# Stacked two-pass scores, masks combined later, a shorter gate series and later attention parts in a one-core hybrid layer

## The chip, the cores and the metric

The kernel runs on one core of one Trainium2 chip. The metric is the device time of one execution in microseconds (us). Before the change it was 987.21, 987.92 and 988.73 us in three runs, with a median of 987.92.

## The reference

One layer serves a prompt of 512 rows and a sample group of 64 rows (576 columns in all) with the same weights, D = 1024:

```python
h = x + concat(gated_delta(n), diff_attention(n)) @ w_out      # n = rmsnorm(x), one projection n @ w_in feeds both
h = h + mem_attention(rmsnorm(h), mem_k, mem_v)                # mem_k, mem_v = rmsnorm(mem) @ w_mem_k, w_mem_v
h = h + square(relu(rmsnorm(h) @ w_ff1)) @ w_ff2
```

Two pieces matter for the change. The gates of the gated-delta part are g = -exp(a_log) * softplus(a + dt_bias) and beta = sigmoid(b). In the differential attention, each of 4 heads has two components c of width 64; a query of component c meets the keys of component c, two softmaxes result, and a = p0 - lam * p1 multiplies the values. Queries come in blocks of 128 and see the keys up to the end of their own chunk of 64. The sample rows see 256 cached keys and their own 64.

## The kernel before

The work is transposed: features lie on the 128 partitions, tokens (576) in the free dimension. `project` (L162 to L165 belong to its weight loading) multiplies 128 columns of weights with all tokens. To keep fp32 accuracy, `split_weights` divides the weights `raw` into a rounded part `wh` (ACT, L161) and a rest `wl` (DVE, L162), both fp32r, and activations are divided likewise; a product is three fp32r matmuls, issued by `mm` (L107) into a PSUM bank `pr`. `tr` (L113) transposes on TensorE. Banks: `pr` has 3, `ba` 2, `g0`, `g1` and `gs` one each, so that a matmul into `g0` waits until all readers of the last content of `g0` are done.

The stages, in time order: norm of x; projection and convolution of 12 blocks of gated-delta inputs (to about 105 us; evacuation in `conv_input`, L322 and L323; Silu at L459 and L460); gates (L507 to L590); the remaining projection `z`, with five chunks of the gated-delta recurrence woven in (to about 250 us; Silu of `z` at L647 and L649); differential attention (to about 355 us); memory K and V, output projection, memory attention, feed-forward (to the end).

The gates: L507 gathers `ab2`, L522 to L526 form t = exp(-|pre|), L527 to L534 a series for log(1 + t), L535 to L538 give `gg`. Triangular matmuls turn `gg` into cumulated sums `Gc`, `kdc` (an exp at L571) and `kdc2` (L590). A DRAM round trip (`gdram` L577, `grow` L582) gives rows of the sums broadcast over the partitions.

`gdn_prep` prepares a chunk: transposes of k into `g0` or `g1`, `kd` from them (DVE, L680), their squares (ACT, L682) and sums (DVE, L683); the same for q (L686, L687), a power on GpSimd (`rpow`, L208), decays `Y` from `grow` or from a matmul (L700, exp at L701), then `At` (L705), `KQ` (L709) and `vb` (L717). It uses `lev`, a matrix of powers of two made from seven masks (L605 to L614; three GpSimd instructions and two DVE instructions for each mask).

`diff_project` projects q, k and v of a head. q goes into `qz`, 128 rows by 2 components, with zeros in the rows of the other component; so a score is one fp32 matmul of `qz` with all 128 rows of k (`kdT`), in `diff_head`, L1019 being the maximum of a row. `finish` norms a head's output into `od`, which is split into `ob` (L201, L202) behind the memory keys.

The order of each engine's instructions is fixed at build time by the framework's scheduler, which takes the code's order as priority and its own estimates of durations; tile buffers, their counts and `issue_after` bound it. Weights come over SP's DMA queue in the order that it was given too. Two of ScalarE's functions, exp and Silu, use different tables; where they alternate, the compiler puts an ACT_TABLE_LOAD between.

Of the kernel before, what the change touches and what calls it, by code (L numbers as in the profile page):

```python
# [15 lines left out]
P = 128  # L16
D = 1024
KT = 8
SEQ = 512
# [18 lines left out]
def hybrid_layer_kernel(  # L38
# [53 lines left out]
    def small(tag, shape, bufs=None, dt=F32):  # L92
        tag = SHARED.get(tag, tag)
        bufs = 1 if tag in ("vn", "on", "S") or tag[:-1] in ("At", "Dt", "Y") else 2
        return sp.tile(shape, dt, tag=tag, name=nm(tag), bufs=bufs)
# [216 lines left out]
    def conv_input(m, tag="cb"):  # L312
# [3 lines left out]
        def evac(b, a0, n, more):  # L316
# [4 lines left out]
            else:  # L321
                A.copy(cb[:, 3 + a0 : 259 + a0], b[:, :256])  # L322
                V.tensor_copy(cb[:, SOFF + 3 : SOFF + 3 + DEC], b[:, 256:])  # L323
# [206 lines left out]
    V.tensor_scalar(t3, t2, 1.0 / 17, 1.0 / 15, ALU.mult, ALU.add)  # L530
    for d in (13, 11, 9, 7, 5, 3, 1):
        V.tensor_tensor(t3, t3, t2, ALU.mult)
        V.tensor_scalar(t3, t3, 1.0 / d, None, ALU.add)
    V.tensor_tensor(t3, t3, t1, ALU.mult)  # L534
# [64 lines left out]
    with tc.issue_after(behind_keys[0]), tc.issue_after(behind_keys[1]):  # L599
        lev = const([P, P], "lev")  # L600
        prev = ident
        for lb in range(7):
            s = 2 << lb
            e = small("X", [P, P])
# [4 lines left out]
            m = small("B0", [P, P])  # L609
            V.tensor_tensor(m, e, prev, ALU.subtract)  # L610
            if lb == 0:
                V.tensor_copy(lev, m)
            else:
                V.scalar_tensor_tensor(lev, m, float(1 << lb), lev, ALU.mult, ALU.add)  # L614
            prev = e
# [323 lines left out]
    qz = [cp.tile([P, 2, T], F32, tag=f"qz{i}", name=f"qz{i}") for i in range(2)]  # L939
    with tc.issue_after(behind_keys[0]), tc.issue_after(behind_keys[1]):  # L940
        for q2 in qz:
            G.memset(q2[64:, 0, :], 0.0)
            G.memset(q2[:64, 1, :], 0.0)
        G.memset(vs[64:], 0.0)

    def diff_project(h):
        hs = slice(h * P, (h + 1) * P)
        for kind, base in (("q", 2056), ("k", 2568), ("v", 3080)):
            def evac(b, a0, n, more):
                ts_ = slice(a0, a0 + n)  # L950
                if kind == "q":
                    for c in range(2):
                        R = slice(64 * c, 64 * c + 64)
                        if more is not None:
                            add_to(qz[h % 2][R, c, ts_], b[R], more[R])
                        else:
                            (A.copy if c else V.tensor_copy)(qz[h % 2][R, c, ts_], b[R])
                    return
# [664 lines left out]
```

## Time and profile before

| | |
|---|---|
| time, three runs | 987.21, 987.92, 988.73 us |
| profiled execution | 987.2 us |
| its span | 985.5 us |
| TensorE busy | 968.5 us (98%) |
| DVE busy | 699.7 us (71%) |
| ACT busy | 530.1 us (54%) |
| granted TensorE clock | 0.997 |

Times in the trace are from the start of the span; about 1.7 us of the execution lie outside it. PE is TensorE, DVE VectorE, ACT ScalarE, POOL GpSimd, SP SyncE. A row of the timeline has its start, its duration, engine, line, operation, out<-in, shape, the number of instructions merged, and in brackets how long the engine had stood idle before it and what it waited for. PE's durations overlap; what counts is the distance of starts.

### The profile page before, as it was taken

To read this page: it belongs to the slowest core of one execution; us is meant where nothing else is said; L and a number is where in the kernel's file an instruction comes from. 1 tells how busy PE (TensorE), PEld (TensorE's weight loads), DVE (VectorE), ACT (ScalarE), POOL (GpSimd) and SP (SyncE) were. 2 spreads that over 40 slices of the span, in tenths; PEclk is the share of its full clock that TensorE was granted. 3 is DMA by queue.
4 is the path that set the end of the run, shared out by engine and by line. 5 is a ranking of instruction groups with operands and counts; after the bars stand their busy time and mean duration, and the time that the engine had idled before them with its cause. 6 is when DMAs were issued, how large, how long until landed. Compare 5 with 4: busy or idle time off the path is not lost.

```text
span 985.5 us, 16923 instructions
## 1 busy us (share of the span) xinstructions
PE 968.5 (98%) x6403; PEld 891.2 (90%) x6403; DVE 699.7 (71%) x1570; ACT 530.1 (54%) x1194; POOL 58.8 (6%) x127
## 2 busy tenths in 40 slices
PE   9999999999999999999999999999999999999996
PEld 7989899898888878999999999999999999999996
DVE  6666787877676676666557977657867779978674
ACT  7545575344656665444445657665544445555444
POOL 3341011101000000000000000000000000000000
PEclk9999999999999999999999999999999999999998
DMA  7432340103222647333111414222222223223202
GB/s 212 129 119 65 90 138 23 43 23 103 81 68 68 203 131 227 95 94 99 44 44 58 127 54 127 86 86 86 86 87 86 86 86 86 86 86 86 65 23 96
DMA packets 121714, 90.75 MB, mean 92 GB/s; under 512 B 5564, under 2 KB 112206, under 8 KB 121122
## 3 DMA queue, kind: packets, MB, share of 16 engines
q1 hardware_dynamic: 121266, 89.03, 30.9%
q8 instruction: 50, 0.82, 0.3%
q10 hardware_dynamic: 368, 0.66, 0.2%
q14 instruction: 30, 0.25, 0.1%
HBM read 79.93 MB, written 9.75 MB: 91 GB/s over the span
## 4 chain that ended last, share of the span: by engine, by line
PE 83%; DVE 4%; issue 3%; POOL 2%; DMA 2%; ACT 2%; POOLq 0%; ACTq 0%; SPq 0%; DVEq 0%
PE pr L107 51%; PE g L107 12%; PE ba L107 10%; PE gs L107 6%; PE ba L113 3%; PE g L113 1%; POOL tg L208 1%; DMA r<-in_w_ff_dram 1%; DVE p L457 1%; DVE wl L162 0%; DMA grow<-gdram 0%; DMA raw<-in_w_ff_dram 0%; POOL X L607 0%; POOL X L608 0%; DVE on L809 0%
## 5 line engine op out<-in xcount | busy, mean ns | idle before, releaser
L107 PE MATMUL pr<-u,wh 128*128 128x320 f32 (+2 forms) x1240 | 328.7, 343 | 1.3 <-DVE p L323 1.2
L107 PEld LDWEIGHTS pr<-u,wh 128*128 128x128 f32 x1240 | 212.3, 188 | 18.0 <-DVE p L323 1.8
L107 PE MATMUL pr<-u,wl 128*128 128x256 f32 (+1 forms) x816 | 226.7, 302 | 0.0
L107 PEld LDWEIGHTS pr<-u,wl 128*128 128x128 f32 x816 | 149.9, 189 | 2.7 <-DVE wl L388 0.2
L162 DVE TENSOR_TENSOR wl<-raw,wh 128x1024 fp32r<-128x1024 f32 x65 | 79.4, 1223 | 41.3 <-ACT wh L161 41.0
L161 ACT CAST wh<-raw 128x1024 fp32r<-128x1024 f32 x65 | 68.1, 1048 | 65.7 <-PE pr L107 50.5
L107 PE MATMUL pr<-u,w2h 128*128 128x320 f32 (+1 forms) x384 | 98.5, 340 | 0.0
L1369 ACT CAST w2h<-r 128x512 fp32r<-128x512 f32 x56 | 34.7, 620 | 87.9 <-PE pr L107 85.3
L107 PE MATMUL pr<-f,w2h 128*128 128x320 f32 (+1 forms) x288 | 74.3, 340 | 0.1
L107 PEld LDWEIGHTS pr<-u,w2h 128*128 128x128 f32 x384 | 65.0, 188 | 4.5 <-ACT u L1452 0.3
L107 PE MATMUL pr<-u,w2l 128*128 128x256 f32 (+1 forms) x256 | 65.1, 295 | 0.0
L1454 DVE TENSOR_TENSOR u<-u,pr 128x256 f32<-128x256 f32 x96 | 42.3, 448 | 16.9 <-PE pr L107 16.2
L107 PE MATMUL ba<-u,wl 128*128 128x288 f32 x360 | 53.0, 296 | 0.4 <-ACT keep L1405 0.4
L107 PEld LDWEIGHTS pr<-f,w2h 128*128 128x128 f32 x288 | 48.7, 188 | 4.0 <-issue 1.1
L107 PEld LDWEIGHTS ba<-u,wl 128*128 128x128 f32 x360 | 49.2, 188 | 1.2 <-ACT keep L1405 1.1
L107 PE MATMUL pr<-f,w2l 128*128 128x256 f32 (+1 forms) x192 | 48.8, 295 | 0.0
L107 PEld LDWEIGHTS pr<-u,w2l 128*128 128x128 f32 x256 | 46.9, 188 | 1.5
L208 POOL TENSOR_TENSOR tiny<-tiny,nhalf 128x1 f32<-128x1 f32 (+4 forms) x10 | 8.7, 870 | 631.6 <-DVE tiny L1522 529.8
L1370 DVE TENSOR_TENSOR w2l<-r,w2h 128x512 fp32r<-128x512 f32 x56 | 38.5, 688 | 10.7 <-ACT w2h L1369 10.4
L107 PE MATMUL pr<-wh,u 128*128 128x512 f32 x128 | 41.4, 401 | 0.0
L1414 ACT ACTIVATE c<-c 128x288 f32<-128x288 f32 x48 | 20.6, 443 | 29.5 <-DVE c L1413 29.5
L107 PEld LDWEIGHTS pr<-f,w2l 128*128 128x128 f32 x192 | 35.2, 188 | 1.2
(514 smaller groups left out, 2025.1 us busy)
## 6 DMA issues: line engine op xcount, KB each, us to landing
raw<-in_w_ff_dram SPq DMA_DIRECT2D x36, 512.0 KB
raw<-in_w_in_dram SPq DMA_DIRECT2D x28, 512.0 KB
r<-in_w_ff_dram SPq DMA_DIRECT2D x56, 256.0 KB
raw<-in_w_mem_k_dram SPq DMA_DIRECT2D x8, 512.0 KB
raw<-in_w_mem_v_dram SPq DMA_DIRECT2D x8, 512.0 KB
raw<-in_w_out_dram SPq DMA_DIRECT2D x8, 512.0 KB
raw<-in_w_mem_q_dram SPq DMA_DIRECT2D x8, 512.0 KB
raw<-in_w_mem_o_dram SPq DMA_DIRECT2D x8, 512.0 KB
```

Of the source, the lines that this page charges most:

```text
L107: i = nc.tensor.matmul(out, lhsT, rhs, start=start, stop=stop, skip_group_check=skip_group_check)
L113: i = nc.tensor.transpose(out, in_, ident[:n, :n])
L161: A.copy(wh, raw)
L162: V.tensor_tensor(wl, raw, wh.bitcast(F32), ALU.subtract)
L208: G.tensor_tensor(out, in_, bc(nhalf[: in_.shape[0], 0:1], list(in_.shape)), ALU.pow)
L457: V.scalar_tensor_tensor(yv[:, :n], cb[:, i : i + n], cwt[:, m, i : i + 1], yv[:, :n], ALU.mult, ALU.add)
L1369: A.copy(wh, src)
L1370: V.tensor_tensor(wl, src, wh.bitcast(F32), ALU.subtract)
L1414: A.activation(c, c, AF.Relu)
L1454: V.tensor_tensor(am, am, b, ALU.add)
```

## The change

Five edits go together. Scores of the prompt are made by two fp32r matmuls: the rounded part and the rest of q stand in the upper and lower 64 rows of `qs`, and one component's k, rounded part and rest, each stand twice, in both halves of the partitions; the stacking is done by DMAs from SBUF to SBUF, and the buffers are taken from tags that are free by then. `qz` holds only the last 128 columns, for the sample rows. The small evacuation at L323 moves to ACT. The gates' series loses seven instructions. The masks of `lev` are made ahead in two `X` tiles, and are combined later, with 7 DVE instructions in place of 14. The split of the attention output into `ob` stands in the code behind the first half of the memory values.

```diff
@@ -91,7 +91,7 @@
 
     def small(tag, shape, bufs=None, dt=F32):
         tag = SHARED.get(tag, tag)
-        bufs = 1 if tag in ("vn", "on", "S") or tag[:-1] in ("At", "Dt", "Y") else 2
+        bufs = 1 if tag in ("vn", "on", "S", "qz") or tag[:-1] in ("At", "Dt", "Y") else 2
         return sp.tile(shape, dt, tag=tag, name=nm(tag), bufs=bufs)
 
     def tiny(shape, tag="tiny", bufs=16):
@@ -320,7 +320,7 @@
                 add_to(cb[:, 3:259], b, more)
             else:
                 A.copy(cb[:, 3 + a0 : 259 + a0], b[:, :256])
-                V.tensor_copy(cb[:, SOFF + 3 : SOFF + 3 + DEC], b[:, 256:])
+                A.copy(cb[:, SOFF + 3 : SOFF + 3 + DEC], b[:, 256:])
 
         return evac
 
@@ -527,11 +527,10 @@
     V.reciprocal(t2, t2)
     V.tensor_tensor(t1, t1, t2, ALU.mult)
     V.tensor_tensor(t2, t1, t1, ALU.mult)
-    V.tensor_scalar(t3, t2, 1.0 / 17, 1.0 / 15, ALU.mult, ALU.add)
-    for d in (13, 11, 9, 7, 5, 3, 1):
-        V.tensor_tensor(t3, t3, t2, ALU.mult)
-        V.tensor_scalar(t3, t3, 1.0 / d, None, ALU.add)
-    V.tensor_tensor(t3, t3, t1, ALU.mult)
+    V.tensor_scalar(t3, t2, 1.0 / 17, None, ALU.mult)
+    for d in (15, 13, 11, 9, 7, 5, 3):
+        V.scalar_tensor_tensor(t3, t3, 1.0 / d, t2, ALU.add, ALU.mult)
+    V.scalar_tensor_tensor(t3, t3, 1.0, t1, ALU.add, ALU.mult)
     V.tensor_scalar(pre, pre, 0.0, None, ALU.max)
     V.scalar_tensor_tensor(t3, t3, 2.0, pre, ALU.mult, ALU.add)
     V.tensor_tensor(t3, t3, ea.unsqueeze(1).to_broadcast([P, 5, 4]), ALU.mult)
@@ -596,23 +595,19 @@
     mn = view(e5, 0, 2, D)
     mhl = pair(4, F32R)
     mh, ml = view(mhl, 0, KT, NMEM), view(mhl, 1, KT, NMEM)
-    with tc.issue_after(behind_keys[0]), tc.issue_after(behind_keys[1]):
-        lev = const([P, P], "lev")
-        prev = ident
-        for lb in range(7):
+    near_ = [t for u in (small("X", [P, 4, P]), small("X", [P, 4, P])) for t in (u[:, 0, :], u[:, 1, :], u[:, 2, :])]
+    with tc.issue_after(behind_keys[1]):
+        for lb, e in enumerate(near_):
             s = 2 << lb
-            e = small("X", [P, P])
             G.memset(e, 1.0)
             ev = e.rearrange("p (n s) -> p n s", s=s)
             G.affine_select(out=ev, in_=ev, pattern=[[-s, P // s], [0, s]], compare_op=ALU.is_ge, fill=0.0, base=0, channel_multiplier=1)
             G.affine_select(out=ev, in_=ev, pattern=[[s, P // s], [0, s]], compare_op=ALU.is_ge, fill=0.0, base=s - 1, channel_multiplier=-1)
-            m = small("B0", [P, P])
-            V.tensor_tensor(m, e, prev, ALU.subtract)
-            if lb == 0:
-                V.tensor_copy(lev, m)
-            else:
-                V.scalar_tensor_tensor(lev, m, float(1 << lb), lev, ALU.mult, ALU.add)
-            prev = e
+    lev = const([P, P], "lev")
+    with tc.issue_after(last_v):
+        V.tensor_scalar(lev, ident, -1.0, 64.0, ALU.mult, ALU.add)
+        for lb, e in enumerate(near_):
+            V.scalar_tensor_tensor(lev, e, -float(1 << lb), lev, ALU.mult, ALU.add)
 
 
 
@@ -936,31 +931,62 @@
     cv2 = view(e3, 1, 4, 4 * P).rearrange("p (i b) n -> p i b n", i=2)
     ckT, cvv = cv2[:, 0].rearrange("p b (c n) -> p (b c) n", n=PAST), cv2[:, 1]
 
-    qz = [cp.tile([P, 2, T], F32, tag=f"qz{i}", name=f"qz{i}") for i in range(2)]
+    qs = [cp.tile([P, 2, T], F32R, tag=f"qz{i}", name=nm("qs")) for i in range(2)]
+    qz = small("qz", [P, 2, P])
     with tc.issue_after(behind_keys[0]), tc.issue_after(behind_keys[1]):
-        for q2 in qz:
-            G.memset(q2[64:, 0, :], 0.0)
-            G.memset(q2[:64, 1, :], 0.0)
+        G.memset(qz[64:, 0, :], 0.0)
+        G.memset(qz[:64, 1, :], 0.0)
         G.memset(vs[64:], 0.0)
+    stacked = {}
 
     def diff_project(h):
         hs = slice(h * P, (h + 1) * P)
+        if h < 2:
+            qn = [od[:, 2 * h + j, :SEQ].bitcast(F32R) for j in range(2)]
+        else:
+            qn = [small(tag, [P, SEQ], dt=F32R) for tag in ("Y0", "Y1")]
+        tags = ("kd", "vb", "X", "KQ") if h % 2 else ("At0", "At1", "Dt0", "Dt1")
+        ks = [small(tag, [P, SEQ], dt=F32R) for tag in tags]
+        stacked[h] = ks[:2], ks[2:]
         for kind, base in (("q", 2056), ("k", 2568), ("v", 3080)):
             def evac(b, a0, n, more):
                 ts_ = slice(a0, a0 + n)
+                t0 = slice(a0, min(a0 + n, SEQ))
+                n0 = t0.stop - a0
+
+                def parts(dst, src):
+                    A.copy(dst[0][:, t0], src[:, :n0])
+                    V.tensor_tensor(dst[1][:, t0], src[:, :n0], dst[0][:, t0].bitcast(F32), ALU.subtract)
+
                 if kind == "q":
-                    for c in range(2):
-                        R = slice(64 * c, 64 * c + 64)
-                        if more is not None:
-                            add_to(qz[h % 2][R, c, ts_], b[R], more[R])
-                        else:
-                            (A.copy if c else V.tensor_copy)(qz[h % 2][R, c, ts_], b[R])
+                    d = b
+                    if more is not None:
+                        d = qn[1][:, ts_].bitcast(F32)
+                        add_to(d, b, more)
+                    parts(qn, d)
+                    if a0:
+                        for c in range(2):
+                            R = slice(64 * c, 64 * c + 64)
+                            A.copy(qz[R, c, :], d[R, n - P :])
+                            for j in range(2):
+                                nc.sync.dma_start(
+                                    qs[h % 2][64 * j : 64 * j + 64, c, :SEQ].bitcast(F32), qn[j][R].bitcast(F32)
+                                )
                     return
                 d = small("zr", [P, 320])[:, :n] if kind == "v" else kdT[:, h, ts_]
                 if more is not None:
                     add_to(d, b, more)
                 else:
                     V.tensor_copy(d, b)
+                if kind == "k":
+                    parts(stacked[h][0], d)
+                    if a0:
+                        first_, second_ = ([x.bitcast(F32) for x in pair_] for pair_ in stacked[h])
+                        for j in range(2):
+                            for R in (slice(0, 64), slice(64, P)):
+                                nc.sync.dma_start(second_[j][R], first_[j][64:])
+                        for j in range(2):
+                            nc.sync.dma_start(first_[j][64:], first_[j][:64])
                 bt = bank()
                 for t in range(2):
                     tr(bt[:, t * P : (t + 1) * P], d[:, t * P : (t + 1) * P])
@@ -1005,22 +1031,22 @@
             q0 = QT[t][0]
             nk = q0 + P if t < 4 else PAST + DEC
             nb = (nk + P - 1) // P
-            pr = []
+            pr = {}
             mx, l = tiny([P, 2], "ta"), tiny([P, 2], "ta")
-            for c in range(2):
+            for c in (1, 0):
                 b = bank(f"g{c}")
-                qq = qz[h % 2][:, c, q0 : q0 + P]
                 if t < 4:
-                    mm(b[:, :nk], qq, kdT[:, h, :nk])
+                    for j in range(2):
+                        mm(b[:, :nk], qs[h % 2][:, c, q0 : q0 + P], stacked[h][c][j][:, :nk], start=j == 0, stop=j == 1)
                     V.memset(b[:64, nk - 64 : nk], -1e30)
                 else:
-                    mm(b[:, :PAST], qq, ckT[:, h, :])
-                    mm(b[:, PAST:nk], qq, kdT[:, h, SEQ:T])
+                    mm(b[:, :PAST], qz[:, c, :], ckT[:, h, :])
+                    mm(b[:, PAST:nk], qz[:, c, :], kdT[:, h, SEQ:T])
                 V.tensor_reduce(mx[:, c : c + 1], b[:, :nk], AX.X, ALU.max)
                 V.tensor_scalar(mx[:, c : c + 1], mx[:, c : c + 1], -0.125, None, ALU.mult)
                 p = small(f"p{c}", [P, 512])
                 A.activation(p[:, :nk], b[:, :nk], AF.Exp, bias=mx[:, c : c + 1], scale=0.125, accum_out=l[:, c : c + 1])
-                pr.append(p)
+                pr[c] = p
             V.reciprocal(l, l)
             V.tensor_tensor(l[:, 1:2], l[:, 1:2], nlam, ALU.mult)
             V.tensor_scalar(pr[1][:, :nk], pr[1][:, :nk], l[:, 1:2], None, ALU.mult)
@@ -1109,7 +1135,7 @@
             nc.sync.dma_start(out[0, 0].rearrange("(b p) h d -> p b (h d)", p=P)[:, :, fs], dst[:, :, fs])
             if out is o_mk and f == 1:
                 finish()
-
+            if out is o_mv and f == 0:
                 ob = pair(5, F32R)
                 for h in range(H):
                     split_to((ob,), od[:, h, :], h, 0)
```

New line numbers in the gates and in `gdn_prep` are 1 lower (L570 for L571, L589 for L590) and 5 lower (L675 for L680, L695 for L700).

The first place is DVE around the gates. In `gg_1158` and the like the last number is a tile's own. Before, from the last step of the series on:

```order
L537 TENSOR_TENSOR t3_1162<-t3_1162,tiny_136_1155 128x20
L538 TENSOR_SCALAR gg_1158<-t3_1162 128x20
L545 COPY gg2_1191<-gg_1158 64x2 x2
L548 MEMSET gg_1158 64x4
L568 COPY Gc_1233<-ba_143_1230 128x20
...
L570 TENSOR_TENSOR kdc_1235<-ba_143_1230,Gc_1233 128x20
...
L680 TENSOR_TENSOR kd_167_1315<-g0_166_1310,kdc_1235 128x512
L680 TENSOR_TENSOR kd_208_1485<-g1_207_1480,kdc_1235 128x512
L162 TENSOR_TENSOR wl_272_1851<-raw_270_1848,wh_271_1850 128x1024
L683 TENSOR_REDUCE tg_165_1309<-B0_168_1317 128x4
L700 SCALAR_TENSOR_TENSOR Y1_213_1503<-grow_146_1246,Gc_1233,most1_1101 128x128 x2
```

After, the same stretch, from the end of `gg` on:

```order
L537 TENSOR_SCALAR gg_1158<-t3_1162 128x20
...
L547 MEMSET gg_1158 64x4
...
L569 TENSOR_TENSOR kdc_1228<-ba_143_1223,Gc_1226 128x20
L162 TENSOR_TENSOR wl_260_1822<-raw_258_1819,wh_259_1821 128x1024
L695 SCALAR_TENSOR_TENSOR Y1_201_1474<-grow_146_1239,Gc_1226,most1_1101 128x128 x2
L675 TENSOR_TENSOR kd_155_1286<-g0_154_1281,kdc_1228 128x512
L675 TENSOR_TENSOR kd_196_1456<-g1_195_1451,kdc_1228 128x512
...
L678 TENSOR_REDUCE tg_153_1280<-B0_156_1288 128x4
L682 TENSOR_REDUCE tg_153_1280<-B0_158_1296 128x4
...
L707 TENSOR_TENSOR tg_167_1333<-tg_153_1280,tg_152_1279 128x4
...
L695 SCALAR_TENSOR_TENSOR Y0_161_1309<-g0_160_1304,Gc_1226,most1_1101 128x128 x4
```

`kd` stood ahead of the decays `Y1` from `grow` and now stands behind the first two of them; the decays `Y0` stand behind L707, which reads GpSimd's power.

The second place is ACT behind the gates. Before:

```order
L549 ACT_TABLE_LOAD
L549 ACTIVATE t1_1160<-ab_1150 128x20
L569 ACTIVATE egl_1234<-ba_143_1230 128x20
L571 ACTIVATE kdc_1235<-kdc_1235 128x20
L590 ACTIVATE kdc2_1194<-kdc2_1194 128x2
L161 CAST wh_271_1850<-raw_270_1848 128x1024
L682 ACTIVATE B0_168_1317<-g0_166_1310 128x512
```

After:

```order
L568 ACTIVATE egl_1227<-ba_143_1223 128x20
L589 ACTIVATE kdc2_1187<-kdc2_1187 128x2
L644 ACT_TABLE_LOAD
L644 ACTIVATE u_2_76<-pr_247_1686 128x64
L161 CAST wh_259_1821<-raw_258_1819 128x1024
L570 ACT_TABLE_LOAD
L570 ACTIVATE kdc_1228<-kdc_1228 128x20
L194 COPY u_2_76<-pr_251_1719 128x256
L642 ACT_TABLE_LOAD
L642 ACTIVATE u_2_76<-pr_252_1739 128x256
L677 ACTIVATE B0_156_1288<-g0_154_1281 128x512
```

The exps of `egl`, `kdc` and `kdc2` stood together behind one table load; now Silu's of `z` stand between them and in front of the squares `B0`, each change with a load. From the gates' first exp (L525) to the end of the first chunk's `At` there are 12 loads, where there were 6.

The third place is SP's DMA queue where head 0 and head 1 of the differential attention meet. `At0`, `At1` hold head 0's k (component 0, rounded part and rest), `Dt0`, `Dt1` component 1; `kd_516`, `vb_517`, `X_518`, `KQ_519` are the same for head 1. Before:

```order
L977 DMA out_2_dram<-p0_455_2694 128x2x128
L980 DMA out_8_dram<-p0_455_2694 64x128
L990 DMA p0_468_2773<-in_cache_diff_k_dram 128x512
L1179 DMA B0_884_4940<-in_cache_mem_v_dram 128x512
L988 DMA u_2_76<-in_cache_diff_v_dram 128x2x512
```

After:

```order
L989 DMA At1_434_2550<-At1_434_2550 64x512
L1014 DMA u_2_76<-in_cache_diff_v_dram 128x2x512
L987 DMA Dt0_435_2551<-At0_433_2549 64x512 x2
L987 DMA X_518_2955<-kd_516_2953 64x512
L1009 DMA out_3_dram<-u_4_78 128x4x128
L1010 DMA out_9_dram<-vs_2542 64x128
L989 DMA At0_433_2549<-At0_433_2549 64x512
L987 DMA X_518_2955<-kd_516_2953 64x512
L987 DMA KQ_519_2956<-vb_517_2954 64x512 x2
L157 DMA raw_684_3762<-in_w_in_dram 128x8x128
```

The copies of k stand between the outputs and the weights; head 0's last copy stands behind the first copy of head 1.

## The prediction

> **What bounds the kernel.** I read the page first: busy shares, then the chain that ended last.
>
> ```profile
> PE 968.5 (98%) x6403; PEld 891.2 (90%) x6403; DVE 699.7 (71%) x1570; ACT 530.1 (54%) x1194; POOL 58.8 (6%) x127
> ...
> PE 83%; DVE 4%; issue 3%; POOL 2%; DMA 2%; ACT 2%; POOLq 0%; ACTq 0%; SPq 0%; DVEq 0%
> ```
>
> TensorE works 98% of 985.5 us and carries 83% of the chain. So two things alone move the time: matmul time, and moments in which TensorE stands still. Next the stages that the change touches (columns: PE, weight load, DVE, ACT, POOL busy), and TensorE's waits there (total, times, longest).
>
> ```profile
> 102.00:118.00 16.00, 15.54 (x103) 13.61 (x103) 12.53 (x44) 9.03 (x15) 0.00 (x0) 1.00 0.42 113
> 117.00:135.00 18.00, 17.36 (x120) 15.76 (x121) 14.60 (x47) 14.19 (x27) 3.32 (x2) 1.00 0.49 156
> 250.00:355.00 105.00, 104.06 (x610) 86.45 (x609) 72.64 (x239) 62.95 (x207) 4.78 (x7) 1.00 0.32 99
> ```
>
> ```profile
> PE pr L107 <- DVE p L323: 1.2, 2, 1.0
> ...
> PE pr L107 <- DVE wl L162: 0.8, 1, 0.8
> ...
> PE g L113 <- DVE KQ L709: 0.5, 1, 0.5
> ...
> PE ba L107 <- DVE gg L548: 0.5, 1, 0.5
> ```
>
> In the differential-attention stage (250 to 355) TensorE idles 0.9 us of 105: matmul time saved there counts in full. In the gate stage (102 to 135) it idles 1.1 us, with DVE at about 80% and ACT at 79% of 117 to 135: there little room is left, and whatever makes their results late stops TensorE.
>
> **Part 1, the scores: -7.1 us.** The score matmuls now run in fp32 and become two fp32r matmuls with stacked halves.
>
> ```profile
> 264.88 0.28 PE L107 MATMUL pr<-u,wl 128*128 128x256 f32 x1
> 265.00 0.40 PE L107 MATMUL pr<-u,wh 128*128 128x512 f32 x1
> 265.24 0.40 PE L107 MATMUL pr<-u,wl 128*128 128x256 f32 x2
> ...
> 265.71 1.04 PE L107 MATMUL g<-u,qz 128*128 128x512 f32 x2
> 266.58 0.38 PE L113 MATMUL ba<-ident,p 128*128 128x128 f32 x2
> ```
>
> ```profile
> L107 PE MATMUL g<-u,qz 128*128 128x512 f32 x16 | 8.4, 609 | 0.0
> L107 PE MATMUL g<-u,qz 128*128 128x384 f32 x16 | 7.0, 519 | 0.0
> ```
>
> One fp32 matmul is two instructions (the form of 512 columns has 16 for 8 matmuls). From start to start the pair takes 0.87 us (265.71 to 266.58), 0.85 ns per column and instruction; an fp32r instruction of 512 columns takes 0.24 us and one of 256 0.12 (265.00 to 265.24, 264.88 to 265.00), 0.46 ns per column. The new form has as many instructions, so it saves 0.39 ns per column: 16 x (512+384+256) columns x 0.39 = 7.1 us. For t=0 (128 columns) I count nothing: bounds 0 and 16 x 128 x 0.39 = 0.8 us. The sample scores (t=4) stay fp32.
>
> The price is paid elsewhere: per head two more casts and two subtractions for q and k each, and two copies into `qz`.
>
> ```profile
> L194 ACT COPY zr<-pr 128x256 f32<-128x256 f32 x12 | 4.5, 374 | 10.1 <-PE pr L107 10.1
> ...
> L195 DVE TENSOR_TENSOR zr<-pr,zr 128x256 f32<-128x256 f32 x12 | 5.1, 422 | 2.5 <-ACT zr L194 2.3
> ```
>
> That is 4 x 0.37 on ACT and 4 x 0.42 on DVE per head, less what the old evacuation took, some 5 us and 3 us in all; against 42 and 32 us free in 250 to 355 it is hidden, and without that cover it would cost these 8 us. New too are 40 copies from SBUF to SBUF on SP's queue. Their landing isn't in this trace; the nearest rows:
>
> ```profile
> 118.45 0.28 SPq L577 DMA_DIRECT2D gdram<-p  x1
> 119.77 0.35 SPq L582 DMA_DIRECT2D grow<-gdram  x1
> ...
> 123.81 0.62 DVE L700 SCALAR_TENSOR_TENSOR Y<-grow,Gc,most 128x128 f32<-128x128 f32 x2 [0.91 <-DMA grow<-gdram]
> ```
>
> 10 KB had landed 1.3 us after issue, 256 KB 4.0 us after. Tightest is head 0: its last k copy stands on SP behind head 1's first (the third pair of order blocks shows it), which waits for head 1's k. From that evacuation 1.3 us, four issues of 0.4 and a landing make 4.2 to 6.9 us; the matmuls that stand before its first score take 7.4. The other copies that it waits for can add a landing. Behind these copies SP still has the next weights to fetch (`raw_684`), which are first split well over 4.0 us later and wait no longer than the scores do. So 0 to 1.6 us, and I take 0.5, nearer the covered end, as the order leaves room.
>
> **Part 2, the conv evacuation: -1.2 us.** The 64-column copy moves from DVE to ACT.
>
> ```profile
> 57.56 1.22 DVE L162 TENSOR_TENSOR wl<-raw,wh 128x1024 fp32r<-128x1024 f32 x1
> ...
> 58.69 0.22 DVE L323 COPY p<-pr 128x64 f32<-128x64 f32 x1
> ...
> 58.97 0.50 PE L107 MATMUL pr<-u,wh 128*128 128x512 f32 x1 [1.04 <-DVE p L323]
> ```
>
> It stood behind a weight split and masks' subtractions; ACT is idle there, so both waits (1.2 in all) go. Masks now need no subtraction and stand later. The lower bound is 0.2, should ACT's own queue be late.
>
> **Part 3, attention parts later: -0.3 us.** The one wait on `wl` in the memory stage:
>
> ```profile
> 361.80 1.42 DVE L202 TENSOR_TENSOR u<-u,u 128x576 fp32r<-128x576 f32 x2
> 363.14 2.35 DVE L162 TENSOR_TENSOR wl<-raw,wh 128x1024 fp32r<-128x1024 f32 x2
> ```
>
> The wait is 0.8 us behind those splits. In the new order three of four splits still stand ahead of a `wl` that TensorE reaches after 6.1 us of matmuls instead of 5.9, so most of it stays: 0 to 0.8, I take 0.3.
>
> **Part 4, the gate stage: +7.8 us.** Here the order changes most. T is the moment at which `gg` is ready.
>
> ```profile
> 106.15 0.24 DVE L507 COPY ab<-ba 128x80 f32<-128x80 f32 x1 [0.30 <-PE ba L113]
> ...
> 111.60 0.18 DVE L532 TENSOR_TENSOR t<-t,t 128x20 f32<-128x20 f32 x1
> 111.81 0.18 DVE L533 TENSOR_SCALAR t<-t 128x20 f32<-128x20 f32 x1
> ...
> 117.04 0.06 DVE L548 MEMSET gg<- 64x4 f32 x1
> ```
>
> ```profile
> 117.16 0.40 PE L107 MATMUL ba<-gg,triu 128*128 128x20 f32 x2 [0.46 <-DVE gg L548]
> ...
> 135.10 0.60 PE L113 MATMUL g<-ident,X 128*128 128x128 f32 x4
> ```
>
> The series loses 7 instructions of 0.21 us (111.60 to 111.81), 1.5 us; `lev` puts 7 of about 0.29 in, three quarters of which fall into gaps in which DVE waited for ACT. `gg` comes 10.1 us after L507 instead of 10.95. But TensorE reaches it 13 matmuls of 320 columns earlier (0.46 ns x 320 = 0.147 each, 1.9 in all): it waits 0.46 + 1.9 - 0.9 = 1.5 us.
>
> Behind T, ACT alternates between exp and Silu, each time with a table load:
>
> ```profile
> 108.44 1.28 ACT L525 ACT_TABLE_LOAD   x1
> 109.73 0.22 ACT L525 ACTIVATE t<-t 128x20 f32<-128x20 f32 x1
> ...
> 118.75 0.22 ACT L571 ACTIVATE kdc<-kdc 128x20 f32<-128x20 f32 x1 [0.53 <-DVE kdc L570]
> 119.89 0.20 ACT L590 ACTIVATE kdc<-kdc 128x2 f32<-128x2 f32 x1 [0.93 <-DVE kdc L589]
> 120.00 1.04 ACT L161 CAST wh<-raw 128x1024 fp32r<-128x1024 f32 x1
> ```
>
> Before, `kdc` was there at T+1.9 (118.97). Now it follows `kdc2` (T+2.8), a load (1.28), a Silu (0.2), a cast (1.04), a load and its exp: T+6.8. On DVE its user, `kd`, stands moreover behind `Y1`, which waits for `grow` at T+6.7 (123.81 less 117.10) and takes 0.6: both `kd` end at T+8.6 instead of T+4.0. On ACT a copy, a third load and a Silu put the k squares at T+9.4. TensorE needs that bank at T+7.0 (matmuls between by the pitches above): **2.4 us**. A fourth load puts the q squares at T+12.2, sums and POOL's power at T+14.9:
>
> ```profile
> 125.20 0.17 DVE L688 TENSOR_SCALAR tg<-tg 128x8 f32<-128x8 f32 x1
> ...
> 127.14 0.16 DVE L712 TENSOR_TENSOR tg<-tg,tg 128x4 f32<-128x4 f32 x1 [0.42 <-POOL tg L208]
> ```
>
> (1.94 us between the two). `Y0`'s four decays, now behind that step, end at T+16.2, wanted at T+14.9: **1.3**. The scaled memory rows (L233), behind the second pair of sums and POOL, end at T+19.8, wanted at T+17.7: **2.1**. `At0`'s last part stands behind a `wl` (1.2): T+22.2 against T+20.8: **1.4**. `KQ` at T+24.7 against T+23.0: **1.7**. Together 8.9, with `gg` 10.4, less the 0.9 that stood here before: 9.5. Adding starts instead: TensorE is at `gg` at 116.7 - 1.2 - 1.9 = 113.6, waits 1.5, and 26.2 us behind T reaches the transposes of `X` that stood at 135.10. There it has ten matmuls of `pr_261` (five of 512 columns, five of 256) and two of 320 more still to do, 2.05 us, but eight transposes (0.9) less: 113.6 + 1.5 + 26.2 + 1.15 - 135.1 = 7.3, or 8.5 without part 2's 1.2. In such hand sums some waits cover one another, so I take 7.8; bounds 3.5 (`kd` and the squares alone, 2.4, with `gg`'s rise of 1.1) and 10.
>
> [...]
>
> **Sum.** -7.1 + 0.5 - 1.2 - 0.3 + 7.8 = -0.3. The profiled execution took 987.2 us (span 985.5 and 1.7 around it): 986.9. The median of the runs, 987.92, is 0.7 above it: 987.6. The bounds of the terms give -7.1 -0.8 -1.2 -0.8 +3.5 = -6.4 (981.5) and -7.1 +1.6 -0.2 +10 = +4.3 (992.2).
>
> **Rivals.**
> - *The gate waits cover one another* (faster). If TensorE's first stop lets DVE and ACT catch up, only the lower bound, 3.5, is left: -7.1 + 0.5 - 1.2 - 0.3 + 3.5 = -4.6, **983.3**. For it: 32 us of DVE free later. Against: all five waits stand behind each other in order.
> - *The copies land late* (slower). If an SBUF copy takes 4.0 us, and the stacking of k is two such steps, every head's first scores wait: 1.6 for head 0 and 1.5 each for three: +6.1 instead of 0.5, **993.2**. It decides from about 3 us a landing on. For it: the 256 KB row; against: these are 128 KB, and the scores stand well behind the projections.
> - *A switch costs more than its load.* Four switches stand on the path behind T; were each as dear as two loads, 4 x 1.28 = +5.1, **992.7**. Against: 108.44 to 109.73. [...]
> - *The fp32r pair saves nothing*, because weights are loaded anew for each: **994.7**. Against: the `pr` rows load anew too, at 0.24.
>
> **How the numbers follow.** Forecast 0.45, covering rival 0.27, late copies 0.18, dear switches 0.05, no saving 0.05. The forecast's own range is 985 to 991. A measurement of this kernel tells 0.2%, 2 us, from no change: below 985.9 is faster, above 989.9 slower. Of the forecast 0.08 lies below, 0.27 within, 0.10 above. Faster 0.27 + 0.08 = 0.35; same 0.27; slower 0.10 + 0.28 = 0.38. The range of 8 in 10 takes in both neighbours: 981.5 to 994.
>
> **What would show it.** Score rows of 512 columns at 0.24 us a piece; no wait on L323; a wait of 1 to 2 us on `gg`; twelve table loads in the gate stage; waits on `B`, `Y`, `u`, `At` and `KQ` in some 27 us behind `gg`. Wrong, if TensorE's idle time from `gg` on grows by less than 4 us, or if scores wait for SP's copies.

## The result and the profile after

The changed kernel takes **989.86 us** (median of 11 runs, 988.37 to 991.83); the kernel before, beside it, 987.70 (11 runs, 986.23 to 988.73). The ratio is 1.0026, interval 1.0017 to 1.0034: 2.2 us slower, where 0.3 us less was forecast. The profiled execution took 988.73 us with a span of 986.7 (before 987.2 and 985.5).

The page first: TensorE's busy time, and its share of the chain that ended last.

```profile
PE 964.3 (98%) x6403; PEld 891.3 (90%) x6403; DVE 696.1 (71%) x1552; ACT 544.6 (55%) x1228; POOL 56.4 (6%) x122
...
PE 88%; DVE 3%; issue 2%; ACT 2%; DMA 2%; POOL 1%; POOLq 0%; SPq 0%; ACTq 0%; DVEq 0%
```

TensorE works 4.2 us less than before (968.5) in a span 1.2 us longer, so it stands still some 5 us more. Where, its waits between 100 and 150 us say (in total, times, longest):

```profile
PE g L113 <- ACT B L677: 3.0, 1, 3.0
PE ba L113 <- DVE u L233: 1.4, 1, 1.4
PE g L107 <- DVE At L700: 1.1, 1, 1.1
PE g L113 <- DVE KQ L704: 0.9, 1, 0.9
```

Before, this stretch held two waits of 0.5. None on `gg`, none on `Y0` is among the four, and no wait on L323 is left in the kernel. The windows of the gate stage (columns: PE, weight load, DVE, ACT, POOL busy, then the granted clock, the DMA's share and GB/s), before:

```profile
118.00:140.00 22.00, 21.52 (x155) 20.11 (x155) 19.02 (x58) 17.11 (x34) 3.88 (x3) 1.00 0.47 146
```

and after:

```profile
118.00:140.00 22.00, 15.65 (x99) 13.95 (x98) 15.32 (x42) 19.72 (x31) 3.84 (x3) 0.92 0.48 144
123.00:124.00 1.00, 0.01 (x1) 0.01 (x1) 1.00 (x3) 0.66 (x2) 0.00 (x0) 0.97 1.05 422
124.00:125.00 1.00, 1.00 (x5) 0.83 (x5) 1.00 (x4) 0.98 (x2) 0.00 (x0) 0.50 0.99 362
...
126.00:127.00 1.00, 1.00 (x6) 1.00 (x5) 0.00 (x1) 1.00 (x3) 0.00 (x0) 0.50 0.50 116
127.00:128.00 1.00, 1.00 (x7) 1.00 (x7) 0.93 (x3) 1.00 (x2) 0.03 (x1) 0.82 0.04 9
```

TensorE is idle for 6.35 of the 22 us (before 0.48), as its busy 15.65 says (before 21.52). And something is there that no part of the prediction has: from about 123.95 to 127.4 the granted clock is 0.50. Four transposes with 128 columns each took 0.91 us to the next start there (123.99 to 124.90) and 0.46 at 1.00 (138.59 to 139.05), twice the time; so a busy TensorE did in these 3.4 us what takes 1.7 at 1.00. The busy column, which stays at 1.00, doesn't show it: the clock's column does.

How the 3.0 us wait comes about, on ACT, DVE and PE:

```profile
115.96 0.19 ACT L568 ACTIVATE egl<-ba 128x20 f32<-128x20 f32 x1
116.04 0.20 ACT L589 ACTIVATE kdc<-kdc 128x2 f32<-128x2 f32 x1
116.24 1.28 ACT L644 ACT_TABLE_LOAD   x1
117.54 0.23 ACT L644 ACTIVATE u<-pr 128x64 f32<-128x64 f32 x1
118.27 1.05 ACT L161 CAST wh<-raw 128x1024 fp32r<-128x1024 f32 x1 [0.51 <-ACT u L644]
119.34 1.28 ACT L570 ACT_TABLE_LOAD   x1
120.63 0.22 ACT L570 ACTIVATE kdc<-kdc 128x20 f32<-128x20 f32 x1
...
122.62 1.28 DVE L675 TENSOR_TENSOR kd<-g,kdc 128x512 f32<-128x512 f32 x2
123.34 1.20 ACT L677 ACTIVATE B<-g 128x512 f32<-128x512 f32 x2 [0.53 <-DVE kd L675]
...
123.99 1.12 PE L113 MATMUL g<-ident,u 128*128 128x128 f32 x4 [2.98 <-ACT B L677]
```

The exp of `kdc` had its input at 116.4 and runs at 120.63, behind two table loads, a Silu and a cast; `kd`, the squares and TensorE follow.

A second count says what the rest of the kernel did. For every TensorE instruction I took the distance to the next start, less the median distance of its form in the same run; summed by stretch (us), this is idle time and slow clock together:

| stretch | before | after | change |
|---|---|---|---|
| 0 to 40 | 3.4 | 4.0 | +0.6 |
| 40 to 80 | 2.7 | 0.9 | -1.8 |
| 80 to 120 | 1.1 | 0.6 | -0.5 |
| 120 to 140 | 1.0 | 9.0 | +8.0 |
| 140 to 260 | 10.7 | 11.0 | +0.3 |
| 260 to 380 | 8.6 | 7.4 | -1.2 |
| 380 to the end | 8.5 | 9.2 | +0.7 |

That is +6.1. The matmuls themselves, by their medians, became 4.8 us shorter, nearly all of it the scores: 6.1 - 4.8 = +1.3, the span's growth of 1.2. So the time goes into 20 us, the gate stage.

The scores after (first a pair of 512 columns with the matmul behind it, then a pair of 128):

```profile
272.79 0.70 PE L107 MATMUL g<-Dt,qs 128*128 128x512 f32 x2
273.32 0.45 PE L107 MATMUL pr<-u,wh 128*128 128x320 f32 x2
...
279.77 0.33 PE L107 MATMUL g<-X,qs 128*128 128x128 f32 x1
279.94 0.27 PE L107 MATMUL g<-KQ,qs 128*128 128x128 f32 x1
280.05 0.52 PE L107 MATMUL pr<-u,wl 128*128 128x320 f32 x2
```

A pair of 512 takes 0.53 us from start to start, where before it took 0.87 and 0.48 was forecast; the pair of 128 takes 0.28, and its first instruction (0.17) is the dear one.

### The profile page after: what moved, and what is told of

Read it like the earlier page. It is cut to its first block, busy times and chain, and to the rows that moved or that the text cites. A ratio compares the mean times of both kernels' runs of the same rounds, so it can differ in the third digit from the quotient of the medians.

```text
span 986.7 us, 17021 instructions
## 1 busy us (share of the span) xinstructions
PE 964.3 (98%) x6403; PEld 891.3 (90%) x6403; DVE 696.1 (71%) x1552; ACT 544.6 (55%) x1228; POOL 56.4 (6%) x122
## 4 chain that ended last, share of the span: by engine, by line
PE 88%; DVE 3%; issue 2%; ACT 2%; DMA 2%; POOL 1%; POOLq 0%; SPq 0%; ACTq 0%; DVEq 0%
PE pr L107 56%; PE g L107 11%; PE ba L107 10%; PE gs L107 6%; PE ba L113 3%; PE g L113 2%; POOL tg L208 1%; DMA r<-in_w_ff_dram 1%; DMA grow<-gdram 0%; DMA u<-in_x_prompt_dram 0%; DMA raw<-in_w_ff_dram 0%; DVE wl L162 0%; ACT c L1441 0%; PE pr L113 0%; DVE tg L682 0%
```

## The experiments

**Theory G**: the loss is the order that the scheduler makes of the gate stage, in which exps and Silus alternate on ACT. It comes from two edits together, the evacuation on ACT and the shorter series; the other edits pay as forecast. Rivals: the loss is in the scores' copies, or in the edits themselves whatever their order, or in the place of `kd` behind `Y1` (K), or in the clock behind the 3 us wait (H); each expectation says which of them it weighs.

### One edit undone

e1 puts the longer series back:

```diff
-    V.tensor_scalar(t3, t2, 1.0 / 17, None, ALU.mult)
-    for d in (15, 13, 11, 9, 7, 5, 3):
-        V.scalar_tensor_tensor(t3, t3, 1.0 / d, t2, ALU.add, ALU.mult)
-    V.scalar_tensor_tensor(t3, t3, 1.0, t1, ALU.add, ALU.mult)
+    V.tensor_scalar(t3, t2, 1.0 / 17, 1.0 / 15, ALU.mult, ALU.add)
+    for d in (13, 11, 9, 7, 5, 3, 1):
+        V.tensor_tensor(t3, t3, t2, ALU.mult)
+        V.tensor_scalar(t3, t3, 1.0 / d, None, ALU.add)
+    V.tensor_tensor(t3, t3, t1, ALU.mult)
```

> The change with the old, longer gate series; all other edits stay. In its order the gate stage has the old 6 table loads and kd ahead of Y1 again. Theory G (the gate stage's new order costs about 8 us and hides the scores' gain): some 8 us below the changed kernel, 980 to 982, 0.992 to 0.994 of before. Rival S (the scores' gain is lost in the differential-attention stage, to the copies and evacuations): no more than 1.5 us from the changed kernel, 988 to 991.

e2 puts the small evacuation back on DVE:

```diff
-                A.copy(cb[:, SOFF + 3 : SOFF + 3 + DEC], b[:, 256:])
+                V.tensor_copy(cb[:, SOFF + 3 : SOFF + 3 + DEC], b[:, 256:])
```

> The change with the 64-column evacuation back on DVE; all other edits stay, the short series too. In its order the gate stage has 6 table loads and kd ahead of Y1. Theory G: the gate stage's 8 us come back, less up to 1.2 us of waits on L323: 981 to 983. Rival C (the shorter series itself, with the masks in it, makes the stage slow): 988 to 991, as the changed kernel.

Measured: e1 981.09 us (ratio 0.9934, 0.9919 to 0.9949), e2 **980.43** (0.9927, 0.9912 to 0.9942), the fastest kernel of this study. The gate stage of e2, by its windows:

```profile
40.00:65.00 25.00, 24.96 (x166) 22.97 (x166) 16.16 (x27) 16.72 (x32) 14.64 (x41) 1.00 0.47 159
...
118.00:140.00 22.00, 21.67 (x163) 20.57 (x162) 20.19 (x54) 17.85 (x36) 4.84 (x4) 1.00 0.48 144
```

Either edit undone brings the gate stage back (21.67 busy; e1 21.02) and the whole kernel to 6.4 and 7.1 us below before. The other row is worth a look: 40 to 65 has no wait in e2 either, with L323 on DVE. Its waits went because the masks no longer work there, not because of ACT.

### The scores taken out, and alone

e3 keeps all but the scores, e4 has them alone. The core of the edit:

```diff
-                    for j in range(2):
-                        mm(b[:, :nk], qs[h % 2][:, c, q0 : q0 + P], stacked[h][c][j][:, :nk], start=j == 0, stop=j == 1)
+                    mm(b[:, :nk], qq, kdT[:, h, :nk])
```

> The change without its stacked scores (fp32 scores, no copies); all other edits stay, and the gate stage has the changed kernel's 12 table loads. Theory G, with a gain of 7 us from the scores: 995 to 998, 1.008 to 1.010 of before. Rival S (scores gain nothing in all): 988 to 991.

> Before with the stacked scores alone; the gate stage is that of before. Theory G: 980 to 982 (7 us less, with up to 1 us of waits for copies). Rival S: within 1.5 us of before, 986 to 989.

Measured: e3 996.36 us (1.0091, 1.0074 to 1.0108); e4 984.89 (0.9974, 0.9964 to 0.9985). The windows of e3 show the gate stage with its loss, without any new score:

```profile
118.00:140.00 22.00, 15.21 (x97) 13.60 (x96) 14.94 (x41) 19.33 (x30) 3.84 (x3) 0.92 0.46 143
```

The scores are innocent of the loss, and are worth 996.36 - 989.86 = 6.5 us. Alone they gave only 2.6 us. The timeline of e4 shows why:

```profile
246.21 1.89 DVE L202 TENSOR_TENSOR u<-u,u 128x512 fp32r<-128x512 f32 x3
...
248.93 1.23 DVE L162 TENSOR_TENSOR wl<-raw,wh 128x1024 fp32r<-128x1024 f32 x1
250.19 0.42 DVE L195 TENSOR_TENSOR zr<-pr,zr 128x256 f32<-128x256 f32 x1
...
250.67 0.80 PE L107 MATMUL pr<-u,wh 128*128 128x512 f32 x1 [2.85 <-DVE zr L195]
```

Here another order puts splits ahead of an evacuation that TensorE needs, a wait of 2.85 us, with clock 0.50 from 250.7 to 254.1 behind it: 2.85 + 1.7 = 4.6 us, somewhat more than the 3.9 of the 6.5 that are missing. The profiled run, 986.34 us at a mean granted clock of 0.995, is one of the longer of the ten; the three shortest, 983.5 to 983.7, have 0.997, as before has. My expectation (980 to 982) missed since it looked at the gate stage alone.

### The exps held together

e5 is the whole change, in which the Silus, from the second half of the first `z` head on, wait for the exps of `kdc` and `kdc2`:

```diff
-                A.activation(z, b[:, :256], AF.Silu)
-                if a0:
-                    A.activation(zsample[:, h, :], b[:, 256:], AF.Silu)
+                with ExitStack() as later:
+                    if (h, a0) >= (0, 256):
+                        later.enter_context(tc.issue_after(kdc_made))
+                        later.enter_context(tc.issue_after(exps_made))
+                    A.activation(z, b[:, :256], AF.Silu)
+                    if a0:
+                        A.activation(zsample[:, h, :], b[:, 256:], AF.Silu)
```

> The changed kernel with all five edits; only the Silus from the second half of z's first head on are held behind the exps of kdc and kdc2 on ACT. In its order the gate stage has 6 table loads again and kd stands ahead of Y1. Theory G (exps cut apart by Silus make kdc late, and all else follows): TensorE's idle time in 118 to 140 falls from 6.4 to under 1.5 us, and the time to 978 to 981, 0.990 to 0.993 of before. Rival M (the gate stage is slow because the masks' matrix lev and the short series fill DVE there): 986 to 990.

Measured: 983.73 us (0.9960, 0.9946 to 0.9973). Its windows:

```profile
118.00:140.00 22.00, 21.55 (x158) 20.05 (x157) 18.52 (x51) 17.27 (x35) 4.29 (x3) 1.00 0.51 145
240.00:250.00 10.00, 7.35 (x44) 5.42 (x43) 8.44 (x25) 7.24 (x20) 1.16 (x2) 1.00 0.77 235
```

With every edit in place the gate stage is whole again, so it is the order on ACT, not the work. The total missed the expected 978 to 981 and is 3 us above e1 and e2: the new order has waits of its own, 2.65 us in 240 to 250 (on `Y`, `Dt` and a DMA).

### Two rivals inside the gate stage

e6 holds `Y1` behind `kd` and leaves the rest:

```diff
-        for i in range(nb):
-            V.scalar_tensor_tensor(gam[:, i, :], bg[:, i, :], G_[:, i : i + 1], most, ALU.subtract, ALU.min)
+        with tc.issue_after(kd_made) if c == 1 else ExitStack():
+            for i in range(nb):
+                V.scalar_tensor_tensor(gam[:, i, :], bg[:, i, :], G_[:, i : i + 1], most, ALU.subtract, ALU.min)
```

> The changed kernel with one edit of its order: the decays Y1 from grow are held behind kd on DVE; the 12 table loads and TensorE's order stay. Theory G: kdc itself comes only at 120.9, so kd gains at most 1.7 us and the k squares behind Silu 0.5: 988.5 to 990. Rival K (kd behind Y1 is the cause of the late k bank): the wait of 3.0 us on the squares falls to 1 us or less and the clock stays up, 985 to 987.

e7 gives TensorE work in the long wait, 12 matmuls whose result is thrown away:

```diff
+        if c == 0:
+            spare = bank("gs")
+            for _ in range(12):
+                mm(spare[:20, :P], kdc.rearrange("p c h -> p (c h)"), ident)
```

> The changed kernel with 12 idle matmuls of 128 columns (fp32, into the unused bank gs, result thrown away) between the matmuls ahead of the 3.0 us wait and the transposes behind it; they wait for kdc only, so TensorE works for about 2.6 us of the wait. Theory H (TensorE's clock halves after a wait of about 3 us and stays so for 3.4 us, which costs 1.6 us): clock 1.00 behind the wait and 1 to 2 us less than the changed kernel, 988 to 989. Rival N (the low clock costs nothing, since ACT and DVE are late anyway): within 0.5 us of the changed kernel.

Measured: e6 990.70 us (1.0027, 1.0014 to 1.0040), e7 990.60 (1.0029, 1.0019 to 1.0039); both as slow as the whole change. In e6 the wait on the squares shrank by 0.64 us, and a new wait stands behind it:

```profile
123.36 0.66 PE L113 MATMUL g<-ident,u 128*128 128x128 f32 x4 [2.34 <-ACT B L678]
130.33 1.16 PE L107 MATMUL g<-u 128*128 128x128 f32 x8 [1.20 <-DVE Y L697]
```

K wanted 1 us or less to be left of the first wait, and 2.34 are: K falls. The wait for `Y` is not the price of moving `kd`, since e7, which doesn't move it, has the same 1.20 us there (130.30).

In e7 the long wait was filled, the clock stayed at 1.00 until 136.1, and TensorE had its 1.7 us back. It waited them away: 1.20 us for `Y`, where the changed kernel has no wait, and 1.59 for `At` (135.64), where that has 1.07. `KQ` ends 25.1 us behind `gg` in both (112.91 to 138.02 in e7, 113.46 to 138.53 in the changed kernel). So DVE and ACT set the pace here, and the half clock behind the 3.0 us wait cost nothing up to this point. Then, behind these waits, the clock fell to 0.50 after all, for 6.8 us:

```profile
136.00:137.00 1.00, 1.00 (x8) 1.00 (x6) 1.00 (x4) 0.99 (x4) 0.00 (x0) 0.57 0.63 160
...
141.00:142.00 1.00, 1.00 (x7) 1.00 (x6) 0.45 (x1) 0.00 (x0) 0.00 (x0) 0.50 0.03 7
```

That happened in the profiled run. Four of e7's nine runs have a mean granted clock of 0.997 or 0.998, as before has, and took 989.0 to 990.6 us, little different from the changed kernel. So H, which wanted 988 to 989 us, is not borne out for this wait; its rival N (within 0.5 us of the changed kernel) missed by 0.2 us and comes nearer. A half clock behind the later waits is another matter: the ten runs of e6 reach from 987.0 us at a mean clock of 0.996 to 993.0 at 0.990, on the whole longer as the clock is lower.

### The two edits by themselves

e8 has the evacuation and the series, on the kernel before; e10 has the evacuation alone, e11 the series alone (the diffs are those of e1 and e2, turned round).

> Before with two small edits alone: the 64-column evacuation on ACT and the shorter gate series. Its gate stage has the changed kernel's 12 table loads in the order. Theory G: 8 us dearer there, 1.2 us won at L323: 994 to 996. Rival A (the edits add up as each does alone, -1.2 and about 0): 986 to 988.

> The kernel before with only the small evacuation moved to ACT. Its order has 13 table loads (the first exp of kdc behind one Silu), kd ahead of Y1. Theory G: no loss of 7 us can come from it; the waits of 1.2 us on L323 go, the later kdc costs up to that much: 986 to 989 us. Rival (the evacuation alone carries the loss): 994 to 999 us.

> The kernel before with only the shorter series. Its order has 11 table loads, as before, and kd ahead of Y1. Theory G: 986 to 988.5 us, the same as before. Rival (the series alone, which brings gg 1.5 us earlier, carries the loss): 993 to 999 us.

Measured: e8 998.98 us (1.0117, 1.0103 to 1.0131), e10 992.70 (1.0055, 1.0041 to 1.0068), e11 988.69 (1.0014, 1.0004 to 1.0023). In 118 to 140 TensorE is busy 15.56, 21.01 and 21.08 us: only the two together spoil the gate stage. The totals are above my numbers in all three. Of e8's surplus two things are seen: the clock was at 0.50 from 138.2 to 145.0, while TensorE worked for 5.8 us (2.9 us lost, if nothing covers it), and a wait stands at 60 us, which e10 has too:

```profile
60.37 0.39 PE L107 MATMUL pr<-u,wl 128*128 128x256 f32 x1 [1.61 <-DVE wl L162]
```

Where the masks still subtract on DVE, taking L323 away lets them and the weight split trade places, and a wait of 1.6 us stands for the 1.2 that went. The rest of e10's +5.2 lies in small changes of order in many places (by a count like the table's about +1.2 in 160 to 180, +1.7 in 260 to 280, +1.4 from 380 on); which of them it is made of stays open.

### One copy

The scheduler's order turns on little. e9 is the changed kernel with all five edits, but for one of the twelve small copies, the last:

```diff
+        early = len(cbs) < 11
...
-                A.copy(cb[:, SOFF + 3 : SOFF + 3 + DEC], b[:, 256:])
+                (A.copy if early else V.tensor_copy)(cb[:, SOFF + 3 : SOFF + 3 + DEC], b[:, 256:])
```

> The changed kernel, but the evacuation of one of the twelve convolution blocks, the last (a copy of 128x64, 0.2 us, at about 99 us), is left on DVE; the other eleven stay on ACT, and the shorter series and all other edits stay. The order that the scheduler makes of it has 11 table loads in place of 17, and both kd stand ahead of the first Y1 on DVE. Theory G (the loss is that order of the gate stage): TensorE is busy at least 21 us of 118 to 140, the waits on B (3.0), At (1.8), u (1.4) and KQ (0.9) behind gg are gone, and the time is 980 to 982 us. Rival S (the loss is in the parts themselves: eleven copies more on ACT, the series and lev, whatever the order): a copy of 0.2 us changes nothing that can be seen, 989 to 990.5 us, with 15 to 16 us busy in 118 to 140.

Measured: **980.42 us** (0.9936, 0.9923 to 0.9948), as fast as e2 and 9.4 us below the changed kernel, by a copy of 0.2 us on another engine. Its timeline, against the rows of after:

```profile
115.12 0.19 ACT L569 ACTIVATE egl<-ba 128x20 f32<-128x20 f32 x1 [1.70 <-DVE Gc L568]
...
115.84 0.22 ACT L571 ACTIVATE kdc<-kdc 128x20 f32<-128x20 f32 x1 [0.26 <-DVE kdc L570]
...
116.87 1.28 DVE L676 TENSOR_TENSOR kd<-g,kdc 128x512 f32<-128x512 f32 x2
116.99 0.20 ACT L590 ACTIVATE kdc<-kdc 128x2 f32<-128x2 f32 x1 [0.93 <-DVE kdc L589]
117.59 1.20 ACT L678 ACTIVATE B<-g 128x512 f32<-128x512 f32 x2 [0.39 <-DVE kd L676]
...
118.24 0.66 PE L113 MATMUL g<-ident,u 128*128 128x128 f32 x4
...
120.72 1.28 ACT L643 ACT_TABLE_LOAD   x1
```

Its waits between 100 and 150 us, in full:

```profile
PE g L107 <- DVE At L701: 0.3, 1, 0.3
```

`gg` is ready 0.7 us later than in the changed kernel (114.13 against 113.40), and still the exp of `kdc` is 4.8 us earlier, with no table load between the three exps (from 105 to 145 us ACT has 6 loads, as before; the changed kernel has 11); TensorE's transposes start 5.7 us earlier without a wait. In 118 to 140 it is busy 21.66 us; by the count of the table, 120 to 140 holds 0.7 us instead of 9.0. G is shown: the edits are the same, the order differs.

### How long a wait costs the clock

e12 lets TensorE stand still five times in the feed-forward of the kernel before, behind a chain of 1, 2, 3, 4 and 6 powers on GpSimd whose result goes nowhere. The helper (the loop's calls of it are left out here):

```diff
+    def stand_still(n):
+        s, t = bank("gs"), tiny([P, 8])
+        mm(s[:, :4], ident, ones[:, :4], pin=True)
+        with tc.high_priority():
+            A.copy(t[:, :4], s[:, :4])
+            for _ in range(n):
+                rpow(t[:, :4], t[:, :4])
+        mm(s[:, 4:8], ident, t[:, :4], pin=True)
+        return nc.cur_bb.bb.instructions[-1]
```

> The kernel before, in whose feed-forward (TensorE busy 99.9% there at granted clock 1.00) TensorE is made to stand still five times, some 40 us apart: a matmul of 4 columns, a copy of its result on ACT, then 1, 2, 3, 4 and 6 powers in a row on GpSimd (1.24 us each by the rows of L208) and a second matmul of 4 columns that waits for them; the results go nowhere. Estimated waits 2.3, 3.5, 4.8, 6.0 and 8.5 us, 25 in all. Theory H (a wait of about 3 us or more costs its own length and then some 3.4 us at clock 0.50, 1.7 us lost, or twice that): clock 0.50 in the windows behind the four longer ones, none behind the first; 1016 to 1026 us. Rival (the half clock behind the waits of the gate stage comes from something else there; a wait costs only itself): clock 1.00 behind all five, 1010 to 1014 us.

Measured: 1029.33 us (1.0426, 1.0407 to 1.0445), in two runs. The five waits in its timeline:

```profile
656.32 0.59 PE L107 MATMUL gs<-tiny,ident 128*128 128x4 f32 x2 [2.18 <-POOL tiny L208]
...
711.81 0.59 PE L107 MATMUL gs<-tiny,ident 128*128 128x4 f32 x2 [3.35 <-POOL tiny L208]
...
771.02 0.59 PE L107 MATMUL gs<-tiny,ident 128*128 128x4 f32 x2 [4.35 <-POOL tiny L208]
...
828.53 0.59 PE L107 MATMUL gs<-tiny,ident 128*128 128x4 f32 x2 [5.44 <-POOL tiny L208]
...
889.21 0.59 PE L107 MATMUL gs<-tiny,ident 128*128 128x4 f32 x2 [7.86 <-POOL tiny L208]
```

And its windows behind the shortest:

```profile
655.00:656.00 1.00, 0.00 (x0) 0.00 (x0) 0.40 (x1) 0.07 (x1) 1.00 (x1) 1.00 0.00 0
656.00:657.00 1.00, 0.68 (x3) 0.68 (x4) 0.00 (x0) 0.00 (x0) 0.27 (x1) 0.66 0.31 90
657.00:658.00 1.00, 1.00 (x5) 1.00 (x6) 0.00 (x0) 0.00 (x0) 0.00 (x0) 0.50 0.59 173
...
660.00:661.00 1.00, 1.00 (x10) 1.00 (x9) 0.37 (x1) 0.89 (x2) 0.00 (x0) 1.00 0.00 0
```

Already a wait of 2.18 us is followed by half clock, until 659.7; I had expected none there. The clock was 0.50 while TensorE worked for 3.4, 5.9, 4.8, 5.3 and 6.0 us behind the five: 25.4 us at half clock, 12.7 lost at half speed, an estimate (behind the first wait twelve matmuls of 288 columns took 3.0 us, from 656.77, and the next twelve, from 659.77, 1.6). With 23.2 us of waits and 4.1 us of new waits on L1454 and L1456 that makes 40.0 of the 41.9 us; the time came out above the expected 1016 to 1026 by these new waits and the 1.9 us that stay open. The rival, that a wait costs only itself, is out where, as here, TensorE alone sets the pace.

## Why the prediction was wrong

By its own steps, in the profiled executions:

| term | forecast | measured |
|---|---|---|
| scores and their copies, attention parts later | -6.9 | -4.8 in matmul time and -1.2 of idle time in 260 to 380: -6.0 |
| conv evacuation | -1.2 | -1.8 in 40 to 80, +0.6 in 0 to 40: -1.2 |
| gate stage | +7.8 | -0.5 and +8.0: +7.5 |
| not in the sum | 0 | +0.3 in 140 to 260, +0.7 from 380 on: +1.0 |
| sum | -0.3 | +1.3 |

A small gain was forecast and a small loss came. The term that was mis-sized most is **Part 1**, the step that failed: "it saves 0.39 ns per column: 16 x (512+384+256) columns x 0.39 = 7.1 us. For t=0 (128 columns) I count nothing". For t=1 to 3 the pairs went from 15.5 us to 9.9 by their median distances, 5.6 instead of 7.1: those of 256 columns cost the forecast 0.46 ns per column, but many instructions of 384 and 512 took 0.06 to 0.11 us more. For t=0 they went from 1.1 us to 1.9: the bounds there were a further saving of 0 to 0.8 us, and 0.8 were lost. So the term measured -4.8 where -7.1 stood. The mechanism was right, its price per instruction was taken from matmuls that stand in long rows of their kind. That e3 puts the scores at 6.5 us, near the forecast's net of 6.6 (7.1 - 0.5), is in part luck: it holds 1 to 2 us of idle time in 260 to 380, which no term has. The copies land in time: among TensorE's waits of 0.2 us and more none is on a DMA.

**Part 2** was right in size and wrong in its reason. "ACT is idle there, so both waits (1.2 in all) go": e2 has no wait there with the copy on DVE, and e10, with the copy on ACT and the old masks, has one of 1.6 us. The saving belongs to the masks, which the prediction names only beside ACT: that the size came true is luck.

**Part 3**: the wait on `wl` in the memory stage is 0.6 us, 0.2 less; 0.3 was taken.

**Part 4** (T is 113.46 here) named the right places, with sizes that were off in both directions: `gg` 0 instead of 1.5 (it was ready 9.2 us after L507, not 10.1, and TensorE came at 113.51, where 113.6 was forecast), the `k` bank 3.0 instead of 2.4 (`Y1`, ahead of `kd`, had to wait for `grow` until 122.09, T+8.6, where T+6.7 was taken), `Y0` 0 instead of 1.3, L233 1.4 (2.1), `At0` 1.1 (1.4), `KQ` 0.9 (1.7). Those waits add up to 6.4 us, less than the 10.4 of the hand sum. The half clock, 1.7 us, of which the prediction knows nothing, brings them to 8.1. It stands in the place of waits: at full clock, in e7, TensorE waits 1.2 us for `Y`, where 1.3 was forecast. The chain of DVE and ACT was read nearly right, `KQ` at T+25.1 instead of T+24.7; that the parts, off in both directions, add up to within 0.3 of +7.8 is in part luck. ("Wrong, if TensorE's idle time from `gg` on grows by less than 4 us" wasn't met: it grew by 5.9.) By medians the order costs more than in that run, 989.86 - 980.42 = 9.4 us against e9. The runs of the changed kernel reach from 988.4 to 991.8. The profiled one, with 3.4 us of half clock, has a mean granted clock of 0.995, and eight others have 0.994 to 0.996; the two longest, 991.3 and 991.8, have 0.991. So more half clock goes with the longest runs, as in e6; where in those runs it stood was not traced.

So the **sum** missed by 1.6 us in the profile (0.9 in the scores' row, 1.0 in stretches that had no term, 0.3 the other way in the gate stage), and by 2.3 in the medians. What the 1.0 is made of stays open. The rival with the highest chance, waits that cover one another (983.3), is refuted: by the count, 120 to 140 lost 6 us or more in every kernel with this order. No switch cost more than its load: behind each of the eleven loads from 105 to 145 us (1.28 us) the function starts 1.29 or 1.30 us after the load did, as the exp at 120.63 behind the load at 119.34.

What the prediction did not ask was whether this order was a property of the change. It read the order, priced it and added it up, and took the gate's +7.8 as the price of the edits. It hangs on a copy of 0.2 us, and without it the same edits gain 7 us.

## What to carry to other kernels

Where a scheduler fixes the order, an edit's price is its own work plus a new order everywhere: build the change without each part and with each part alone, and look at the order each time, before the sum is made. When exps and Silus alternate on ACT in front of a chain that TensorE waits for, hold them together by hand, and see afterwards what the hold has moved elsewhere. A TensorE that is near 100% busy can pay twice for a wait, as e12 did for 2.18 us, with 3.4 us at clock 0.50 behind it: look at the clock's column there, and then at whether a later wait would have taken the time anyway.

## What the hardware showed

The half clock was not expected. In e12 it began at about 656.3, 710.9, 769.0, 827.0 and 885.0 us, 2.2 to 3.9 us after TensorE had stopped, and stayed for 3.4 us with the wait of 2.18 us, for 6.8 us with those of 3.35, 4.35 and 5.44, and for 10.2 us with that of 7.86. It stayed for 3.4 us in the changed kernel, e3 and e4 too, with waits of 2.98, 3.40 and 2.85 us, and for 6.8 us in e6, e7 and e8. Waits of 1.25 us in the kernel before, 1.61 us in e10 and 1.68 us in e12 left the clock at 1.00. But in these runs length alone doesn't decide: 2.34 us in e6 and 2.79 us in e8 left it at 1.00 as well, while 1.59 us in e7 was followed by half clock (from 136.1). Two waits of 1.4 and 1.1 us, whose ends lie 2.2 us apart, went with half clock in e6 (from 135.5) and e8 (from 138.2), and not in the changed kernel, which has the same two (1.38 and 1.07 us), nor in e3 (1.39 and 1.07). What decides between them was not shown.
